# Routing into expert slots: gathering by the one-hot matrix itself, the norm's factor applied by slot, and the first expert slabs taken by halves

## The chip, the cores and the metric

The kernel runs on one core of one Trainium2 chip. The metric is device time in microseconds of one execution; "before" was run three times, and the median is used. Engines are called TensorE (PE; PEld is its weight load), VectorE (DVE), ScalarE (ACT), GpSimd (POOL) and SyncE (SP), which issues the DMAs.

## The reference, cut to what matters

One encoder layer over 256 tokens of width 1024, all in float32: a first RMSNorm and one wide projection, two attention branches, gates and an output projection, a residual sum. Then the part that this change is about:

```python
h2 = rmsnorm(x, norm_ffn_g)                 # x * rsqrt(mean(x*x) + eps) * gain
group_logits = h2 @ w_router_group + b      # 8 groups
g_sel = argmax(group_logits); w_grp = softmax(group_logits)[g_sel]
exp_logits = (h2 @ w_router_expert + b).reshape(t, 8, 4)
top_vals, top_idx = top_k(exp_logits[g_sel], 2)
combine = one_hot(4 * g_sel + top_idx) * softmax(top_vals) * w_grp
for e in range(32):
    out += (silu(h2 @ w_gate[e]) * (h2 @ w_up[e])) @ w_down[e] * combine[:, e]
x = x + out                                 # and a final RMSNorm
```

The weights of the 32 experts are 96 MB of the 134 MB that the kernel reads.

## The kernel before, in words

The 256 tokens are two tiles of 128 (`t` = 0, 1). The attention half projects with weights split into a high and a low part (three products each, L301 to L303), and ends with `out_product`, whose sums plus the input give `x2` (L809). Weights come in slabs of up to 128 x 2048 float32 (1 MB). Each expert has two slabs for gate and up (the first and the second 512 of the 1024 inputs, `c` = 0, 1), and each group of four experts has four slabs for down, so a group is 12 slabs and all groups are 96. The slabs land in 24 places of SBUF, in order. `take()` (L232) hands out the next slab and issues, on SyncE, the loads whose place has been used up: slab 24 goes where slab 0 was and waits for the last product that reads slab 0.

Routing runs between the attention half and the experts. For each token tile the transposed `x2` is made on TensorE (`turned`, L819) and copied out (L827, L829); eight products per tile give the 40 logits in one PSUM bank per tile (`logits`, L836, banks `lgp[0]` and `lgp[1]`). `inv_root` makes the norm's factor `r2` on VectorE from a square root on ScalarE. `chosen(t)` is a chain of nine small VectorE operations (L850 to L868), each waiting for the one before; its first reads the logits and `r2`, its last gives `sel`, the two chosen experts of each token. Products with a triangle matrix (`cums`, L974, L975, L982) count the tokens ahead of each token at its expert; `place_of` (L879) makes the slot number from it, and `slots` (L884) the one-hot matrix `P_` (tokens by 4 experts x 32 slots) of one group. A second operation (L887) multiplies it by `r2` to `Pr`; it runs on VectorE for group 0, and on GpSimd for the others. `gather` (L902) multiplies `x2` by `Pr`, so a group's tokens come transposed, four of the eight 128-row blocks in each of two banks `gx`; `kept_tokens` (L907) copies them out with the gain.

Then, for each expert, two `gate_up` (L1054: 8 matmuls, shown as 16 instructions) fill one bank, `kept` copies it out (L1060), `hidden` folds it (L1070) and applies Silu (L1075, L1076). After four experts the next group is gathered, `places` (L1019 to L1038) prepares the way back, and four `down` (L1095) and `combine` (L297, L1109) add the group's result to the banks `OA`, which `residual` (L917) has started with `x2`. `heat` (L310) is a product whose result nobody reads; it writes columns 256 to 511 of a bank.

The order on TensorE is the written one from the last output products on (`manual_schedule`, L928). On ScalarE and VectorE it is written by hand in two stretches, L945 to L991 and L1179 on; `in_turn` takes one operation of each of its chains in turn. `weigh` (the combine weights: exponentials on ScalarE, sums on VectorE) is written in the loop, at expert 0. The order of the other engines is made by a planner.

Of the kernel before, what the change touches and what calls it, by code (L numbers as in the profile page):

```python
# [26 lines left out]
CAP = 32  # L27
# [51 lines left out]
def block_kernel(ctx: ExitStack, tc: tile.TileContext, a, out, cap=CAP):  # L79
# [795 lines left out]
    Pr = wk.tile([128, 2, GRP], F32, tag="P0", name="Pr", bufs=1)  # L875
# [5 lines left out]
    def slots(grp, t, eng):  # L881
# [6 lines left out]
        yield  # L888

    def placed(t, cum):  # L890
        place_of(t, cum)
        yield
        yield from slots(0, t, nc.vector)
# [4 lines left out]
    def gather(c, t, p):  # L898

        for k in range(4 * c, 4 * c + 4):  # L900
            kk = k - 4 * c
            nc.tensor.matmul(p[:, kk * GRP:(kk + 1) * GRP], x2[:, t, k * 128:(k + 1) * 128], Pr[:, t],  # L902
                             start=(t == 0 and kk == 0), stop=(t == 1 and kk == 3))

    def kept_tokens(c, p):

        nc.vector.tensor_mul(tokens[c], p.rearrange("p (k s) -> p k s", k=4), bc(g_ffn[:, 4 * c:4 * c + 4], GRP, axis=2))  # L907
# [3 lines left out]
    def residual(i):  # L911

        t, h, c = i // 4, i // 2 % 2, i % 2
        if c == 0:
            OA[t][h] = pa("OA")
        c0 = 256 * c
        nc.tensor.matmul(OA[t][h][:, c0:c0 + 256], ident, x2[:, t, h * 512 + c0:h * 512 + c0 + 256], start=c == 0,  # L917
                         stop=False)

# [25 lines left out]
    urgent.enter_context(tc.manual_schedule(engines={mybir.EngineType.Activation, mybir.EngineType.DVE}))  # L945
# [48 lines left out]
    wts, wg = sm([128, 2, NE], "wts"), sm([128, 2], "wg")  # L994

    def weigh():
        neg = sm([128, 2, 2], "neg")
        nc.vector.tensor_scalar(neg[:, 0], gm, -1.0, None, op0=ALU.mult)
        nc.vector.tensor_scalar(neg[:, 1], m8[:, :, 0], -1.0, None, op0=ALU.mult)
        ge, se = sm([128, 2, NG], "ge"), sm([128, 2], "se")  # L1000
        for t in range(2):
            nc.scalar.activation(ge[:, t], gl[:, t], AF.Exp, bias=neg[:, 0, t:t + 1], accum_out=wg[:, t:t + 1])
            nc.scalar.activation(wts[:, t], el[:, t], AF.Exp, bias=neg[:, 1, t:t + 1])
        for t in range(2):
            nc.vector.scalar_tensor_tensor(wts[:, t], wts[:, t], 1.0, sel[:, t], op0=ALU.mult, op1=ALU.mult,
                                           accum_out=se[:, t:t + 1])
        nc.vector.tensor_mul(se, se, wg)
        nc.vector.reciprocal(se, se)
        for t in range(2):
            nc.vector.tensor_scalar(wts[:, t], wts[:, t], se[:, t:t + 1], None, op0=ALU.mult)  # L1010
# [31 lines left out]
    quarters = [slice(32 * j, 32 * j + 32) for j in range(4)]  # L1042

    def gate_up(n, c, w):
# [134 lines left out]
    with in_order, tc.manual_schedule(engines={mybir.EngineType.Activation, mybir.EngineType.DVE}):  # L1179
        for grp in range(NG):  # L1180
            if grp + 1 < NG:
                for t in range(2):
                    for _ in slots(grp + 1, t, nc.gpsimd):
                        pass
            for e in range(EPG):
# [13 lines left out]
                if n == 0:  # L1199
                    weigh()  # L1200
# [3 lines left out]
                if n == 1:  # L1204
                    for i in range(4, 8):
                        residual(i)
            if grp + 1 < NG:
                for c in range(2):
                    p = pss("gx")
                    for t in range(2):  # L1210
                        gather(c, t, p)
                    kept_tokens(c, p)
            hidden(EPG * grp + EPG - 1)()
            places(grp)()
# [123 lines left out]
```

## Time and profile before

| | us |
|---|---|
| median of three runs | 420.94 (420.42 to 422.38) |
| the profiled execution | 420.53 |
| its span (first to last instruction) | 418.7 |
| TensorE busy | 390.6, 93% of the span |
| VectorE, ScalarE busy | 208.2, 184.4 |
| data read from HBM | 133.4 MB, 321 GB/s over the span |

The table is to be read with the slices over time, since the shares are means over stages of different kinds: a busy TensorE in the attention half and a busy TensorE among the experts need not bound the kernel both. A line of the timeline gives start, duration, engine, line, operation, what it writes and reads, its shape, how many instructions are merged in it, and in brackets how long the engine sat idle before it and what released it. In a merged line the duration runs from the first start to the last end.

### The profile page before, as it was taken

The numbers are of one execution on the slowest core, as the hardware profiler recorded it, in microseconds if no ns is written. First come the engines' busy times: TensorE is split into PE (matmuls) and PEld (weight loads), VectorE is DVE, ScalarE is ACT, GpSimd is POOL, SyncE is SP. The second block draws the span as 40 slices with busy tenths as digits, with TensorE's granted clock in tenths as the row PEclk, the third lists the DMA queues.
The fourth block names the chain that finished last, engine by engine and source line by source line (L and its number), as shares of the span: only waits on it lengthen the run. The fifth ranks groups of instructions, "written<-read, shape, count | busy, mean of one in ns | idle before, by whom it ended". The sixth has DMA issues, their size and how long they took to land.

```text
span 418.7 us, 8153 instructions
## 1 busy us (share of the span) xinstructions
PE 390.6 (93%) x3280; PEld 286.7 (68%) x3280; DVE 208.2 (50%) x554; ACT 184.4 (44%) x403; POOL 27.0 (6%) x30
## 2 busy tenths in 40 slices
PE   7999999999999999999999999999999797797780
PEld 4888887888877878888885757576766373363440
DVE  2989689989869855765571212130303021020023
ACT  4876687668857846565432212212112111111143
POOL 0890000000000000000000010101001001000000
PEclk9999999999999999999999999999999999799996
DMA  7985683649543859589857999999999999999962
GB/s 266 396 359 196 250 310 110 257 160 372 208 160 145 312 206 386 198 312 360 308 229 316 423 419 420 420 422 417 420 420 419 421 420 419 421 420 420 418 259 106
DMA packets 20639, 135.00 MB, mean 322 GB/s; under 512 B 2418, under 2 KB 2930, under 8 KB 5620
## 3 DMA queue, kind: packets, MB, share of 16 engines
q1 hardware_dynamic: 20596, 134.42, 80.9%
q8 instruction: 28, 0.46, 0.5%
q14 instruction: 15, 0.12, 0.1%
HBM read 133.36 MB, written 1.05 MB: 321 GB/s over the span
## 4 chain that ended last, share of the span: by engine, by line
PE 75%; DMA 20%; DVE 2%; ACT 1%; issue 0%; SPq 0%; DVEq 0%; ACTq 0%
DMA w<-in_w_moe 19%; PE a L301 13%; PE a L302 13%; PE a L303 13%; PE G L1054 9%; PE gx L902 5%; PE Y L1095 5%; PE OA L1109 3%; PE G L1070 3%; PE s L318 2%; DMA w<-in_w_att 1%; PE t L543 1%; PE t L455 1%; PE o L603 1%; PE o L659 1%; PE t L647 1%
## 5 line engine op out<-in xcount | busy, mean ns | idle before, releaser
L302 PE MATMUL a<-r 128*128 128x512 f32 (+1 forms) x244 | 93.9, 387 | 0.0
L303 PE MATMUL a<-r 128*128 128x512 f32 (+1 forms) x244 | 92.4, 384 | 0.0
L301 PE MATMUL a<-r 128*128 128x512 f32 (+1 forms) x244 | 83.3, 387 | 1.5 <-ACT r L297 1.5
L1054 PE MATMUL G<-w,tok 128*32 128x256 f32 x1024 | 69.6, 399 | 14.0 <-DMA w<-in_w_moe 14.0
L297 DVE SCALAR_TENSOR_TENSOR r<-w,ident,r 128x512 fp32r<-128x512 f32 (+2 forms) x79 | 62.8, 807 | 15.6 <-ACT r L297 15.3
L297 ACT ACTIVATE r<-w,ident 128x512 fp32r<-128x512 f32 (+2 forms) x79 | 56.9, 750 | 27.1 <-PE a L303 24.8
L1054 PEld LDWEIGHTS G<-w,tok 128*32 128x32 f32 x1024 | 29.7, 112 | 40.3 <-issue 14.6
L301 PEld LDWEIGHTS a<-r 128*128 128x128 f32 x244 | 45.0, 188 | 10.7 <-ACT r L297 2.0
L302 PEld LDWEIGHTS a<-r 128*128 128x128 f32 x244 | 45.9, 188 | 8.6 <-DVE r L297 0.5
L303 PEld LDWEIGHTS a<-r 128*128 128x128 f32 x244 | 45.8, 188 | 8.3 <-issue 0.2
L1076 DVE TENSOR_TENSOR P<-G,P 128x64 f32<-128x64 f32 x32 | 7.2, 225 | 84.3 <-ACT P L1075 84.3
L1075 ACT ACTIVATE P<-G 128x64 f32<-128x64 f32 x32 | 7.2, 224 | 74.5 <-PE G L1070 74.4
L1060 ACT COPY Gs<-G 128x256 f32<-128x256 f32 x32 | 11.9, 372 | 48.4 <-PE G L1054 48.4
L1095 PE MATMUL Y<-w,P 128*32 128x256 f32 x512 | 30.9, 382 | 1.1 <-DMA w<-in_w_moe 1.1
L902 PEld LDWEIGHTS gx<-Pr,x 128*128 128x128 f32 x256 | 29.2, 192 | 3.5 <-issue 3.1
L902 PE MATMUL gx<-Pr,x 128*128 128x128 f32 x256 | 30.7, 278 | 0.2 <-DVE Pr L887 0.2
L297 DVE SCALAR_TENSOR_TENSOR ysb<-Y,ws,ysb 128x512 fp32r<-128x512 f32 (+1 forms) x18 | 12.5, 692 | 36.2 <-ACT ysb L297 19.6
L887 POOL TENSOR_SCALAR Pr<-P,r 128x128 f32<-128x128 f32 x14 | 8.3, 603 | 313.2 <-PE gx L902 188.7
L283 DVE TENSOR_TENSOR r<-w,r 128x512 fp32r<-128x512 f32 x32 | 21.9, 690 | 13.2 <-ACT r L282 10.2
L282 ACT CAST r<-w 128x512 fp32r<-128x512 f32 x32 | 19.8, 620 | 13.7 <-DVE r L283 8.2
L907 DVE TENSOR_TENSOR tok<-gx,ident 128x512 f32<-128x512 f32 x16 | 11.1, 692 | 26.5 <-PE gx L902 26.3
L1070 PEld LDWEIGHTS G<-cst,Gs 128*128 128x128 f32 x128 | 17.5, 199 | 9.8 <-issue 5.3
(222 smaller groups left out, 454.4 us busy)
## 6 DMA issues: line engine op xcount, KB each, us to landing
w<-in_w_moe SPq DMA_DIRECT2D x93, 1024.0 KB, 19.8
w<-in_w_att SPq DMA_DIRECT2D x24, 1024.0 KB, 4.8
w<-in_w_moe SPq DMA_DIRECT2D x6, 512.0 KB, 15.0
w<-in_w_att SPq DMA_DIRECT2D x3, 744.0 KB, 8.7
w<-in_w_att SPq DMA_DIRECT2D x2, 512.0 KB, 5.0
out<-r SPq DMA_DIRECT2D x2, 512.0 KB, 3.3
w<-in_w_att SPq DMA_DIRECT2D x1, 768.0 KB, 6.0
w<-in_w_att SPq DMA_DIRECT2D x2, 372.0 KB, 5.9
```

Source lines behind the costliest of these rows:

```text
L282: nc.scalar.copy(hi, src)
L283: nc.vector.tensor_sub(lo, src, hi.bitcast(F32))
L297: return nc.scalar.mul(hi, ps, g), nc.vector.scalar_tensor_tensor(lo, ps, g, hi.bitcast(F32), op0=ALU.mult, op1=ALU.subtract)
L301: i = nc.tensor.matmul(out_, lh, rh, start=start, stop=False)
L302: nc.tensor.matmul(out_, lh, rl, start=False, stop=False)
L303: nc.tensor.matmul(out_, ll, rh, start=False, stop=stop)
L902: nc.tensor.matmul(p[:, kk * GRP:(kk + 1) * GRP], x2[:, t, k * 128:(k + 1) * 128], Pr[:, t], start=(t == 0 and kk == 0), stop=(t == 1 and ...
L1054: nc.tensor.matmul(G[quarters[2 * z + o], :256], tokens[c][:, kk + o, CAP * e:CAP * e + CAP], w[:, (kk + o) * 512 + z * 256:(kk + o) * 512 ...
L1060: nc.scalar.copy(Gs, G[:, :256])
L1070: nc.tensor.matmul(HT[:, f * 64:(f + 1) * 64], Gs[:, f * 128:(f + 1) * 128], fold, start=True, stop=True)
L1095: nc.tensor.matmul(Y[quarters[e]], hT_[:, e, f], wv[:, f, e], start=f == 0, stop=f == 1)
L1109: nc.tensor.matmul(OA[t][h][:, c0:c0 + w], pl[:, t * 128:(t + 1) * 128], v, start=False, stop=grp == NG - 1 and q0 > 0 and v is lo, skip_g ...
```

## The change

Seven edits, all between the last output product and the second group of experts, but for one that touches every group.

The one-hot matrix is no longer multiplied by `r2`. `gather` uses `P_`; the factor is brought to the slots instead (`factors`: two products `P_` by `r2`, then `spread`: four products that lay it out for the four quarters of a bank), and `kept` of `gate_up` multiplies by it where it copied.

```diff
-        eng.tensor_scalar(Pr[:, t], P_[:, grp % 2, t], r2[:, t:t + 1], None, op0=ALU.mult)
+    rep = cp.tile([128, CAP], F32, name="rep")
+    nc.gpsimd.tensor_add(rep, fold[:, :CAP], fold[:, CAP:])
+    def factors(grp):
+        p = pss("rq")
+        for t in range(2):
+            nc.tensor.matmul(p[:, :1], P_[:, grp % 2, t], r2[:, t:t + 1], start=(t == 0), stop=(t == 1))
+        rd = wk.tile([128, EPG], F32, tag="rd", name="rd")
+        nc.vector.tensor_scalar(rd, own, p[:, :1], None, op0=ALU.mult)
+        def spread():
+            for q in quarters:
+                nc.tensor.matmul(p[q, 4:4 + EPG], rep, rd, start=True, stop=True)
+            rqs[grp] = wk.tile([128, EPG], F32, tag="rq", name="rq")
+            nc.vector.tensor_copy(rqs[grp], p[:, 4:4 + EPG])
+        return spread
-            nc.scalar.copy(Gs, G[:, :256])
+            nc.scalar.mul(Gs, G[:, :256], rqs[n // EPG][:, e:e + 1])
```

`gather` and `kept_tokens` can do a part: some of the blocks, and the slots of some of the experts. The routing's order is rewritten; `weigh` is split into `weigh` (the exponentials) and `weighed` (the sums), and two one-element activations, Exp and Silu, are put ahead of their first use.

```diff
+    root = inv_root(ss2[:, 1, 1:2], D, "n21", early[1], r2[:, 1:2], True)
+    logits(4, 4, 0)
     kept = turned(4, 4, 1, 4)
-    logits(4, 4, 0)
+    residual(0)
+    heat(lgp[0], 1)
     kept()
+    nc.scalar.activation(warm, ones[:, :1], AF.Exp)
     cums = [pt("cum") for _ in range(2)]
-    in_turn(inv_root(ss2[:, 1, 1:2], D, "n21", early[1], r2[:, 1:2], True), chosen(0))
+    chain = chosen(0)
+    next(chain)
+    in_turn(chain, root)
     logits(4, 4, 1)
-    residual(0)
-    residual(1)
-    heat(lgp[0], 6)
+    heat(lgp[0], 4)
...
-    residual(2)
-    residual(3)
-    heat(lgp[0], 5)
-    in_turn(chosen(1))
-    in_turn(placed(0, cums[0][:, :NE]))
+    residual(1)
+    chain = chosen(1)
+    for _ in range(3):
+        next(chain)
+    in_turn(chain, placed(0, cums[0][:, :NE]))
     gx = [pss("gx") for _ in range(2)]
+    gather(0, 0, 0, gx[0])
     nc.tensor.matmul(cums[1][:, :NE], tri, sel[:, 1], start=False, stop=True)
-    heat(lgp[0], 3)
-    gather(0, 0, gx[0])
-    gather(1, 0, gx[1])
+    gather(0, 1, 0, gx[1], 0, 2)
+    heat(cums[0], 2)
     in_turn(placed(1, cums[1][:, :NE]))
-    gather(0, 1, gx[0])
-    gather(1, 1, gx[1])
-    for c in range(2):
-        kept_tokens(c, gx[c])
+    gather(0, 0, 1, gx[0])
+    gather(0, 1, 0, gx[1], 2, 4)
+    weigh()
+    nc.scalar.activation(warm, ones[:, :1], AF.Silu)
+    for i in range(2):
+        kept_tokens(0, gx[0], 2 * i, 2)
```

The first two experts are taken by halves: both first slabs, then both second ones, and the two slabs change places in memory. The rest of the gather, the factors and the other residuals stand between.

```diff
-        off = i * 128 * 2048
+        off = {1: 2, 2: 1}.get(i, i) * 128 * 2048
+            if grp == 0:
+                gate_up(0, 0, take()[1])
+                gather(0, 1, 1, gx[1])
+                for i in range(2):
+                    kept_tokens(1, gx[1], 2 * i, 2)
+                spread = factors(0)
+                gate_up(1, 0, take()[1])
+                spread()
+                kept = gate_up(0, 1, take()[1])
+                for i in range(2, 4):
+                    residual(i)
+                kept()
+                weighed()
+                kept = gate_up(1, 1, take()[1])
+                hidden(0)()
+                kept()
...
-            for e in range(EPG):
+            for e in range(0 if grp else 2, EPG):
```

In the later groups `factors(grp + 1)` stands behind the gather and `spread()` between `hidden` and `places`, and in the loop's first group the slots of group 1 and the residuals 4 to 7 follow the part shown; `slots` of the next group runs on VectorE alone. The order of ScalarE and VectorE is now one stretch from L945 to the end of the loop.

## Rows read from the trace of the kernel before

**Rows 1.** The slices over time of the page: what the DMA engines moved in each of 40 equal parts of the span (10.5 us each).

```profile
GB/s 266 396 359 196 250 310 110 257 160 372 208 160 145 312 206 386 198 312 360 308 229 316 423 419 420 420 422 417 420 420 419 421 420 419 421 420 420 418 259 106
```

**Rows 2.** The chain of waits from its end: start, duration, what the end of the kernel waited for; the first and the last of the four pieces of DMA at its end.

```profile
320.54 19.87 DMA w<-in_w_moe
...
380.22 18.68 DMA w<-in_w_moe
```

**Rows 3.** Half-microsecond windows around the stop of the DMA: length, then the busy time of PE, PEld, DVE, ACT and POOL with the count of instructions in brackets, then the granted TensorE clock, the DMA engines' share and GB/s. The rows from 221.5 and from 229.5 are the first and the last of the 17 windows from 221.5 to 230.

```profile
214.50:215.00 0.50, 0.50 (x6) 0.36 (x4) 0.43 (x5) 0.00 (x0) 0.00 (x0) 1.00 0.93 360
...
216.50:217.00 0.50, 0.50 (x7) 0.50 (x7) 0.39 (x4) 0.33 (x3) 0.00 (x0) 1.00 0.00 0
...
221.50:222.00 0.50, 0.50 (x16) 0.33 (x12) 0.00 (x0) 0.25 (x1) 0.00 (x0) 1.00 0.88 147
...
223.00:223.50 0.50, 0.50 (x10) 0.29 (x12) 0.00 (x0) 0.28 (x1) 0.00 (x0) 1.00 0.99 410
...
229.50:230.00 0.50, 0.50 (x7) 0.46 (x4) 0.00 (x0) 0.00 (x0) 0.00 (x0) 1.00 1.17 492
```

**Rows 4.** The timeline from the gather to the first `down`.

```profile
215.98 3.84 PE L902 MATMUL gx<-Pr,x 128*128 128x128 f32 x32 [0.15 <-DVE Pr L887]
...
218.97 0.69 DVE L907 TENSOR_TENSOR tok<-gx,ident 128x512 f32<-128x512 f32 x1
...
219.75 2.80 PE L1054 MATMUL G<-w,tok 128*32 128x256 f32 x48
...
220.88 20.16 SPq L215 DMA_DIRECT2D w<-in_w_moe  x13
...
223.07 1.07 PE L1054 MATMUL G<-w,tok 128*32 128x256 f32 x16
...
223.22 1.28 ACT L1075 ACT_TABLE_LOAD   x1 [1.09 <-PE G L1070]
...
236.15 3.62 PE L1095 MATMUL Y<-w,P 128*32 128x256 f32 x61
```

**Rows 5.** The chain of waits through the routing.

```profile
208.68 0.82 PE s L836 x8
...
209.50 0.46 PE t L819 x4
...
209.96 0.83 PE s L836 x8
...
224.14 1.06 PE OA L917 x4
```

**Rows 6.** The timeline of the routing.

```profile
205.02 0.42 DVE L829 COPY x2T<-t 128x256 f32<-128x256 f32 x1 [1.36 <-ACT x2T L827]
...
208.71 0.59 ACT L827 COPY x2T<-t 128x512 f32<-128x512 f32 x1 [0.30 <-PE t L819]
...
210.82 0.26 DVE L850 SCALAR_TENSOR_TENSOR lg<-s,r,b_r 128x40 f32<-128x40 f32 x1 [0.47 <-PE s L836]
...
212.80 0.18 DVE L868 TENSOR_SCALAR sel<-el 128x32 f32<-128x32 f32 x1
...
212.89 0.25 DVE L850 SCALAR_TENSOR_TENSOR lg<-s,r,b_r 128x40 f32<-128x40 f32 x1
...
213.15 0.31 PE L974 MATMUL cum<-sel,cst 128*128 128x32 f32 x2
...
214.86 0.18 DVE L868 TENSOR_SCALAR sel<-el 128x32 f32<-128x32 f32 x1
...
215.09 0.41 PE L982 MATMUL cum<-sel,cst 128*128 128x32 f32 x2
```

**Rows 7.** The timeline of `places` of group 0.

```profile
236.12 0.19 PE L1026 MATMUL pl<-sel,cst 128*1 128x32 f32 x1
...
236.35 0.37 ACT L1030 CAST pl<-pl 128x256 fp32r<-128x256 f32 x1 [0.83 <-PE pl L1026]
...
236.76 0.16 DVE L1033 SCALAR_TENSOR_TENSOR wsx<-pl,cst 128x4 f32<-128x4 f32 x1 [0.97 <-ACT pl L1030]
```

**Rows 8.** Single lines of the kernel: duration of one in ns (least, median, most), first and last start, shape.

```profile
L310 PE MATMUL s<-ident_r x14: 272/273/273, 212.5 to 215.6; 128*128 128x256 bf16 x14
...
L884 DVE TENSOR_TENSOR P<-cst,place x16: 281/285/292, 215.2 to 350.6; 128x128 f32<-128x128 f32 x16
...
L1060 ACT COPY Gs<-G x32: 368/372/373, 221.8 to 396.4; 128x256 f32<-128x256 f32 x32
...
L297 ACT ACTIVATE ysb<-Y,ws x18: 473/687/688, 238.1 to 407.8; 128x512 fp32r<-128x512 f32 x14, 128x256 fp32r<-128x256 f32 x4
```

**Rows 9.** The chain of waits at the `down` of group 1.

```profile
256.41 3.59 PE Y L1095 x64
```

**Rows 10.** One-microsecond windows in the last third, with the columns of rows 3.

```profile
332.00:333.00 1.00, 0.00 (x0) 0.00 (x0) 0.00 (x0) 0.04 (x1) 0.00 (x0) 1.00 1.00 418
...
333.00:334.00 1.00, 0.90 (x12) 0.60 (x16) 0.00 (x0) 0.00 (x0) 0.00 (x0) 0.58 1.02 426
...
347.00:348.00 1.00, 0.09 (x4) 0.10 (x8) 0.00 (x0) 0.32 (x1) 0.00 (x0) 1.00 1.00 418
...
348.00:349.00 1.00, 1.00 (x17) 0.42 (x17) 0.00 (x0) 0.00 (x0) 0.00 (x0) 1.00 1.02 426
```

**Rows 11.** The timeline of TensorE at 333.

```profile
333.10 1.94 PE L1054 MATMUL G<-w,tok 128*32 128x256 f32 x16 [1.51 <-DMA w<-in_w_moe]
```

More of the change, by code (lines that the diff above doesn't have):

```diff
@@ L874, in block_kernel, with slots @@
     hT_ = shaped(P_and_hT[:, 4 * GRP:], [128, EPG, 2, CAP])
-    Pr = wk.tile([128, 2, GRP], F32, tag="P0", name="Pr", bufs=1)
+    rep = cp.tile([128, CAP], F32, name="rep")
+    nc.gpsimd.tensor_add(rep, fold[:, :CAP], fold[:, CAP:])
+    rqs = {}
+    quarters = [slice(32 * j, 32 * j + 32) for j in range(4)]
+    def factors(grp):
[10 more added lines that the diff above has]
+        return spread
     def place_of(t, cum):
         nc.vector.scalar_tensor_tensor(place[:, t], cum, 1.0, sel[:, t], op0=ALU.add, op1=ALU.mult)
-    def slots(grp, t, eng):
+    def slots(grp, t):
         dst = P_[:, grp % 2, t].rearrange("p (e s) -> p e s", e=EPG)
@@ L892, in placed, with gather, kept_tokens @@
         yield
-        yield from slots(0, t, nc.vector)
+        yield from slots(0, t)
     tokens = [wk.tile([128, 4, GRP], F32, tag=f"gt{z}", name="tok", bufs=1) for z in range(2)]
-    def gather(c, t, p):
-        for k in range(4 * c, 4 * c + 4):
+    def gather(grp, c, t, p, k0=0, k1=4):
+        for k in range(4 * c + k0, 4 * c + k1):
             kk = k - 4 * c
-            nc.tensor.matmul(p[:, kk * GRP:(kk + 1) * GRP], x2[:, t, k * 128:(k + 1) * 128], Pr[:, t],
+            nc.tensor.matmul(p[:, kk * GRP:(kk + 1) * GRP], x2[:, t, k * 128:(k + 1) * 128], P_[:, grp % 2, t],
                              start=(t == 0 and kk == 0), stop=(t == 1 and kk == 3))
-    def kept_tokens(c, p):
-        nc.vector.tensor_mul(tokens[c], p.rearrange("p (k s) -> p k s", k=4), bc(g_ffn[:, 4 * c:4 * c + 4], GRP, axis=2))
+    def kept_tokens(c, p, e0=0, n=EPG):
+        es = slice(CAP * e0, CAP * (e0 + n))
+        nc.vector.tensor_mul(tokens[c][:, :, es], p.rearrange("p (k s) -> p k s", k=4)[:, :, es],
+                             bc(g_ffn[:, 4 * c:4 * c + 4], CAP * n, axis=2))
     OA = [[None, None], [None, None]]
@@ L944, in block_kernel @@
     urgent.enter_context(tc.high_priority(300))
-    urgent.enter_context(tc.manual_schedule(engines={mybir.EngineType.Activation, mybir.EngineType.DVE}))
+    by_trace = ctx.enter_context(ExitStack())
+    by_trace.enter_context(tc.manual_schedule(engines={mybir.EngineType.Activation, mybir.EngineType.DVE}))
     added(512, 512, 0, acc[1])
@@ L1041, in block_kernel @@
     pls, Gss = {}, {}
-    quarters = [slice(32 * j, 32 * j + 32) for j in range(4)]
     def gate_up(n, c, w):
@@ L1177, in final_part @@
         nc.vector.tensor_mul(ob[:, t, c0:c0 + n], OA[t][h][:, cs], g_fin[0][:, c0:c0 + n])
-    with in_order, tc.manual_schedule(engines={mybir.EngineType.Activation, mybir.EngineType.DVE}):
+    with in_order, by_trace:
         for grp in range(NG):
-            if grp + 1 < NG:
+            if 0 < grp < NG - 1:
                 for t in range(2):
-                    for _ in slots(grp + 1, t, nc.gpsimd):
+                    for _ in slots(grp + 1, t):
                         pass
-            for e in range(EPG):
+            if grp == 0:
[14 more added lines that the diff above has]
+                kept()
+                for t in range(2):
+                    for _ in slots(1, t):
+                        pass
+                for i in range(4, 8):
+                    residual(i)
+            for e in range(0 if grp else 2, EPG):
                 n = EPG * grp + e
@@ L1203, in block_kernel @@
                     todo.pop(0)()
-                if n == 1:
-                    for i in range(4, 8):
-                        residual(i)
             if grp + 1 < NG:
@@ L1210, in block_kernel @@
                     for t in range(2):
-                        gather(c, t, p)
+                        gather(grp + 1, c, t, p)
                     kept_tokens(c, p)
+                spread = factors(grp + 1)
             hidden(EPG * grp + EPG - 1)()
+            if grp + 1 < NG:
+                spread()
             places(grp)()
```

36 lines of the change are left out of this document (17 added, 19 removed).

## The prediction

> **What bounds the kernel now.** I read the 40 slices first. From the 23rd slice on the DMA engines move 417 to 424 GB/s until the last two slices, while they were uneven before that [rows 1]. The chain of waits says the same from its end: from 320.54 to 398.90 it is nothing but waits for expert weights, the first of 19.87 us and the last of 18.68, and only then the last products run [rows 2]. So the second half of the kernel is one saturated stream. It has a start that can be seen. All 24 places of the ring are filled when routing begins to end: the half-microsecond windows show 360 GB/s until 215.0, nothing from 216.5 on, 147 again from 221.5, and full rate from 223.0 [rows 3]. The timeline gives the event that ends the gap: the first `gate_up` runs from 219.75, and SyncE's next expert load is issued at 220.88, behind the last product that read slab 0 [rows 4]. Summing the 17 windows from 221.5 to 230 gives 3.20 MB, which is 7.61 us at 420 GB/s; so the stream counts as full from 222.39, 1.56 us after the release (220.83, just ahead of the issue). Behind it come 72 slabs of 1.049 MB and the final gain of 0.52 MB: 76.0 MB, 181.0 us, and 222.4 + 181.0 = 403.4, where the tail begins. The end therefore moves one for one with the release of slab 0, less whatever the stream starves later. Work of the engines inside the stream is free as long as places come free faster than one per 1.049/0.42 = 2.50 us.
>
> All sums are against the profiled execution, 420.53 us (span 418.7 and 1.83 around it); the median of the runs shown is 420.94, 0.41 above, and the forecast is given on the median.
>
> **The chain to the release, step by step.**
>
> 1. *Logits before transposes.* Before, TensorE went from 209.50 through four transposes (0.46) to `logits(4, 4, 0)`, ending 210.79 [rows 5], and the first op of `chosen(0)` (L850) started at 210.82 [rows 6]. After, the logits go first; their copy (ScalarE, 208.71 + 0.59 = 209.30) [rows 6] is ready, so they end at 209.50 + 0.83 = 210.33. By this alone L850 gains 0.46.
>
> 2. *But an idle product is put between.* `heat(lgp[0], 1)` now stands ahead of `chosen(0)` and writes columns 256 and up of the same PSUM bank that L850 reads in columns 0 to 39. Does L850 wait for it? The trace has the like case: in `places`, ScalarE's copy L1030 reads columns 0 to 255, done by L1019, yet starts at 236.35, just as the products L1026 into columns 272 and up end (236.31); and VectorE's L1033, which reads columns 256 to 259 of that bank, starts at 236.76, released by the end of the ScalarE copy [rows 7]. So this program orders its engines by bank and not by column. The bounds are no wait at all (210.36) and the whole wait; I take the whole wait, since all the rows of this kind show it. TensorE then passes the transposes (0.46), `residual(0)` (two of the four instructions that took 1.06 [rows 5], 0.53) and one idle product (0.27 [rows 8]) before L850: 210.33 + 1.26 + 0.03 = 211.62, which is 0.80 later than before. This is the largest single number of my sum, and it goes against the change.
>
> [...]
>
> 3. *`chosen(0)` and `chosen(1)`.* L850 to the end of L868 takes 2.16 (210.82 to 212.98), with three ops of the second root between already [rows 6]; so the first choice is ready at 213.78, and the second L850 starts 0.09 behind the start of L868, at 213.69. Its own logits don't hold it: the copy behind the transposes ends near 211.4, and eight instructions more take until 212.4.
>
> 4. *First slots early.* Before, VectorE did all nine ops of `chosen(1)` and then the slots, ending with a product by the norm's factor; gather began at 215.98 [rows 4]. After, `cums[0]` is there 0.48 after the choice (212.98 to 213.46), at 214.26; `place_of` slips in behind L857 at 214.5, the slots start 0.22 to 0.3 later at 214.8 and take 0.28 [rows 8]. Gather starts at 215.15, 0.83 earlier. Price: the slots occupy VectorE in front of L862, which could cost nothing or their whole 0.28; I take 0.1, so the second choice is ready at 213.69 + 2.15 + 0.1 = 215.93, 0.89 later than before (215.04).
>
> 5. *Second half.* TensorE does a quarter of the gather (3.84/4 = 0.96) to 216.11, then `cums[1]` (0.41 [rows 6]) to 216.52. VectorE's place and slots take 0.04 + 0.22 + 0.28: 217.1. The quarter that completes `gx[0]` runs to 218.1. Before, both banks had to pass in the order (0,0), (1,0), (0,1), so it ended at 218.86.
>
> 6. *Tokens by halves of the slots.* Before, 0.11 of waiting, one product of 0.69 and 0.09 to TensorE. After, the first half of 256 columns costs about 0.42 (the same size copied from PSUM by VectorE took 0.42 [rows 6]; the ends are half of 0.69 and the whole). 218.1 + 0.11 + 0.42 + 0.09 = 218.7, against 219.75. **The release moves by -1.0 us.** If the first `gate_up` waited for both halves, one more half of at least 0.35 would come on top: -0.65.
>
> **What stands against it later: the first places come free more slowly.** Slab 1 is now the next expert's half, but between the first two `gate_up` stand the last quarter of the gather (0.96) and `factors` (four short products with 128 rows and columns of weights; like the gather's, 0.12 each, 0.48). Release to release is 0.96 + 0.48 + 0.93 (a third of the 2.80 for 48 products) = 2.37, just under the 2.50 that a slab lasts. Up to the first `down` the new work on TensorE is that 1.44, two `spread` of eight instructions (like those of `down`, 61 in 3.62, so 0.47 each), two residuals moved in (0.53 each) and `factors(1)` (0.48): 3.9 in all. Before, this stretch took from 220.83 to 237.05 (16 of the 61 products behind 236.15), 16.2 [rows 4]; after 20.1, and the stream needs the ninth place after 8 x 2.50 = 20.0. So it misses by 0.1, which I take; the lower bound is 0, the upper 0.7 if the instructions in front of VectorE's answers also wait.
>
> **Costed at nothing.** Groups 1 to 7 gain `factors` and `spread`, 0.95 each, 6.7 in all; hidden, since TensorE goes from one group's `down` to the next in 20.3 us (236.15 to 256.41) while 12 slabs take 30 [rows 4, 9]; bounds 0 and 6.7. The 14 GpSimd products vanish; nobody on the chain waited for them. The gate and up copy with a factor may cost 0.47 in place of 0.37 (copies of 128x256 with and without one [rows 8]), on a ScalarE whose results TensorE does not lack: what it waits for there are weights [rows 2]. The table loads, 1.28 each, are off the chain: Silu's at 223.22 delayed ScalarE alone, while TensorE went on with products [rows 4]. The new places have cover too (Exp from 211.4, wanted at 217; Silu from 218.4, wanted at 222); without it each is worth up to 1.28. The weights' sums move past the tokens of group 0, and are needed 15 us later. The swap of two slabs in memory changes the order in which equal transfers come.
>
> **Sum:** -1.0 + 0.1 = -0.9 on 420.53, 419.6; on the median **420.0 us**. About 0.5% (2.1 us) is what a measurement here tells from no change.
>
> **Rivals.**
> - *A: L850 does not wait for the idle product.* Then steps 3 to 6 start 1.25 earlier (210.36), and the release moves by -2.25; with 0.1 of starving, 418.8. For it: the columns are apart, and no row shows this very pair in this order. Against: both waits of [rows 7]. Chance 0.20.
> - *B: the clock falls, slower than before.* Seven idle products and two residuals fewer stand in the routing, and TensorE now waits from 212.9 to 213.9 for the first choice, with a shorter gap at 215. [...] If it fell near 215, the two gather quarters, `cums[1]` and the first `gate_up` (0.96 + 0.96 + 0.41 + 1.0 = 3.3) would take twice that, since 16 instructions of `gate_up` took 1.94 at 333.10 [rows 11] against 1.07 at 223.07 [rows 4]: 420.0 + 3.3 = 423.3. It decides from the point where the clock falls before the release. Against it: one gap of a microsecond, with dense work on both sides. Chance 0.07.
> - *C: the stream starves at the ninth place*, by 1.1, because `spread`, `factors` and the tokens interleave worse than their instructions add up. The gain is eaten: 420.94 - 1.0 + 1.1 = 421.0. For it: the sum leaves 0.1. Chance 0.13.
>
> [...]
>
> **How the numbers follow.** The forecast has 0.60; its own range is 419.4 to 420.7 (the wait of step 2 whole, starving 0 to 0.7, the half token and the slots either way). A and C are taken into the range, B is left out: 418.5 to 421.4. Faster by over 0.5% means under 418.84: half of A and a little of the forecast, 0.14. Slower by over 0.5% means over 423.04: most of B, 0.06. Within: 0.80.
>
> **What would show it.** In the profile after: L850's first start near 211.6 behind an idle product, not 210.4 (step 2 against A); gather from 215.1 in three parts; the first `gate_up` at 218.7; the DMA gap about 1 us shorter; full rate at the ninth place near 239 (against C); granted clock 1.00 from 210 to 225 (against B). I am wrong if the release moves by more than 1.6 or less than 0.4, or if the stream is no longer saturated behind it.

## The result, and the profile after

The changed kernel takes 423.54 us (median of 7 runs, 421.86 to 424.27); the kernel before took 420.51 beside it (420.30 to 422.38). The ratio is 1.0061, 95% interval 1.0043 to 1.0079: slower by 1.8 to 3.3 us; the medians lie 3.0 apart. Forecast were 420.0 and a range of 418.5 to 421.4, with a chance of 0.06 for slower. The profiled execution took 424.17 us, its span 421.9 (2.27 around it); before it was 420.53, 418.7 and 1.83.

The slices of the changed kernel's page, beside [rows 1]: the stream dips in the 24th slice (393, 419 before), and then is steady near 418 in place of 420. The 22nd slice reads 387 where it read 316, but mostly because a slice of the longer span lies 1.7 us later there: in this execution the first load behind the stop is issued at 220.74 us, only 0.14 ahead of the kernel before (220.88).

```profile
GB/s 271 383 372 209 228 298 141 259 169 330 200 200 124 339 212 324 208 361 345 332 149 387 416 393 420 416 419 419 418 419 418 414 419 419 418 419 419 413 192 105
```

Its chain of waits from the end, beside [rows 2]: the same wait for weights, ending 2.75 us later (401.78 against 399.03 in the kernel before, whose line stands second). So 2.75 of the 3.2 us by which this span is longer lie in the stream, or ahead of it, and 0.5 in the tail.

```profile
362.99 19.89 DMA w<-in_w_moe
382.94 18.71 DMA w<-in_w_moe
401.78 0.64 PE Y L1125 x8
```

```profile
399.03 0.64 PE Y L1095 x8
```

The timeline of the routing, beside [rows 4, 6]. This execution runs 0.33 us ahead of that of the kernel before when routing begins (the first transposes behind attention start at 207.74 and 208.07). L851 (L850 before) is released by the idle product L311, as step 2 said. But the first quarter of the gather, 8 instructions, takes 2.05 us, twice the 0.96 that a quarter took before, and the first `gate_up` comes at 219.61 and not at 218.7.

```profile
210.84 0.27 PE L311 MATMUL s<-ident_r 128*128 128x256 bf16 x1
211.15 0.26 DVE L851 SCALAR_TENSOR_TENSOR lg<-s,r,b_r 128x40 f32<-128x40 f32 x1 [1.34 <-PE s L311]
...
213.41 0.38 PE L1021 MATMUL cum<-sel,cst 128*128 128x32 f32 x2 [0.65 <-PE s L311]
...
214.84 2.05 PE L920 MATMUL gx<-P,x 128*128 128x128 f32 x8 [0.16 <-DVE m8s L863]
...
219.61 1.07 PE L1084 MATMUL G<-w,tok 128*32 128x256 f32 x16
```

One-microsecond windows of that stretch (columns as in [rows 3]) say why: the granted clock falls to 0.50. In the four microseconds from 211 to 215, in the last of which it falls, TensorE was busy for 0.87, 0.76, 0.59 and 0.84.

```profile
211.00:212.00 1.00, 0.87 (x8) 0.76 (x7) 0.82 (x7) 0.98 (x2) 0.00 (x0) 1.00 1.00 410
212.00:213.00 1.00, 0.76 (x7) 0.46 (x6) 0.93 (x8) 0.69 (x2) 0.00 (x0) 1.00 1.06 442
213.00:214.00 1.00, 0.59 (x5) 0.62 (x6) 0.86 (x7) 0.00 (x0) 0.00 (x0) 1.00 1.01 426
214.00:215.00 1.00, 0.84 (x4) 0.31 (x4) 0.96 (x6) 0.00 (x0) 0.00 (x0) 0.62 0.64 254
215.00:216.00 1.00, 1.00 (x5) 1.00 (x6) 0.44 (x4) 0.00 (x0) 0.00 (x0) 0.50 0.06 25
...
217.00:218.00 1.00, 1.00 (x7) 0.98 (x8) 0.64 (x4) 0.17 (x1) 0.00 (x0) 0.68 0.00 0
218.00:219.00 1.00, 1.00 (x11) 1.00 (x10) 0.00 (x0) 0.98 (x7) 0.00 (x0) 1.00 0.00 0
```

That is rival B's place, but it turned out not to be the main loss. To compare executions, times below are counted from the first transpose behind attention (208.07 before). "Release" is the first of SyncE's expert loads behind it, "ninth" the ninth, "GB/s" the DMA rate from 255 to 395 us, "end" the end of the span, "around" what the profiled execution took beside its span; the ratio is to the kernel before on the same chip. All columns but the last two come from one profiled execution of each kernel.

| kernel | first gate_up | release | ninth | GB/s | end | around | median us | ratio (95%) |
|---|---|---|---|---|---|---|---|---|
| before | 11.68 | 12.81 | 29.19 | 420 | 210.6 | 1.83 | 420.5 | |
| after | 11.86 | 13.00 | 32.84 | 418 | 214.2 | 2.27 | 423.54 | 1.0061 (1.0043 to 1.0079) |
| e13_again | 10.64 | 11.78 | 31.62 | 418 | 213.0 | 2.23 | 423.93 (one) | |
| e14_again | 10.64 | 11.77 | 31.62 | 418 | 213.3 | 2.29 | 424.19 (one) | |
| e1_heat | 10.59 | 11.72 | 31.56 | 418 | 212.7 | 2.20 | 421.92 | 1.0041 (1.0020 to 1.0063) |
| e2_late | 10.64 | 11.77 | 29.35 | 418 | 211.4 | 2.24 | 422.13 | 1.0049 (1.0031 to 1.0066) |
| e3_both | 10.59 | 11.72 | 29.29 | 418 | 210.6 | 2.14 | 421.30 | 1.0020 (1.0006 to 1.0035) |
| e4_load | 11.67 | 12.81 | 32.68 | 420 | 213.0 | 1.79 | 422.79 | 1.0049 (1.0032 to 1.0066) |
| e5_pad | 11.67 | 12.80 | 29.18 | 418 | 211.6 | 1.84 | 421.68 | 1.0016 (1.0000 to 1.0031) |
| e6_align | 11.67 | 12.80 | 29.18 | 425 | 208.4 | 1.82 | 418.51 | 0.9933 (0.9910 to 0.9955) |
| e7_rep | 10.59 | 11.72 | 29.29 | 420 | 209.8 | 2.22 | 420.38 | 0.9991 (0.9977 to 1.0004) |
| e8_bank | 10.42 | 11.56 | 29.13 | 420 | 209.5 | 2.16 | 420.13 | 0.9982 (0.9965 to 1.0000) |
| e9_afterrep | 10.66 | 11.79 | 31.64 | 420 | 212.6 | 2.12 | 422.37 | 1.0036 (1.0023 to 1.0049) |
| e10_order | 9.75 | 10.88 | 28.45 | 420 | 209.5 | 2.29 | 420.56 | 0.9991 (0.9979 to 1.0003) |
| e11_best | 9.74 | 10.87 | 28.44 | 425 | 206.7 | 1.76 | 418.03 | 0.9933 (0.9919 to 0.9946) |
| e12_pad32 | 11.67 | 12.81 | 29.19 | 420 | 210.7 | 1.81 | 420.84 | 1.0000 (0.9991 to 1.0009) |
| e15_pad160 | 10.64 | 11.77 | 31.62 | 425 | 209.7 | 2.12 | 420.44 | 0.9979 (0.9969 to 0.9989) |
| e16_pad416 | 11.67 | 12.80 | 29.18 | 425 | 208.6 | 1.85 | 418.65 (one) | |
| e17_pad224 | 11.67 | 12.80 | 29.19 | 419 | 210.9 | 1.80 | 420.70 (one) | |

### The profile page after: what moved, and what is told of

Same layout as the page of the kernel before. It is cut to its first block, busy times and chain, and to the rows that moved or that the text cites. A ratio compares the mean times of both kernels' runs of the same rounds, so it can differ in the third digit from the quotient of the medians.

```text
span 421.9 us, 8323 instructions
## 1 busy us (share of the span) xinstructions
PE 395.4 (94%) x3369; PEld 291.5 (69%) x3369; DVE 210.2 (50%) x570; ACT 188.6 (45%) x405; POOL 18.9 (4%) x17
## 4 chain that ended last, share of the span: by engine, by line
PE 59%; DMA 34%; DVE 4%; ACT 1%; issue 1%; SPq 0%; DVEq 0%; ACTq 0%
DMA w<-in_w_moe 32%; PE a L302 12%; PE a L303 12%; PE a L304 12%; PE G L1084 4%; PE gx L920 3%; PE Y L1125 2%; PE s L319 2%; PE OA L1139 1%; DMA w<-in_w_att 1%; PE G L1100 1%; PE t L544 1%; PE OA L937 1%; PE t L456 1%; PE o L604 1%; PE o L660 1%
## 5 line engine op out<-in xcount | busy, mean ns | idle before, releaser
L1084 PE MATMUL G<-w,tok 128*32 128x256 f32 x1024 | 67.1, 388 | 11.2 <-DMA w<-in_w_moe 11.1
L1090 ACT ACTIVATE Gs<-G,rq 128x256 f32<-128x256 f32 x32 | 15.2, 474 | 46.2 <-PE G L1084 46.2
L920 PEld LDWEIGHTS gx<-P,x 128*128 128x128 f32 x256 | 30.6, 198 | 4.0 <-issue 4.0
L920 PE MATMUL gx<-P,x 128*128 128x128 f32 x256 | 32.6, 285 | 0.2 <-DVE m8s L863 0.2
L298 DVE SCALAR_TENSOR_TENSOR ysb<-Y,ws,ysb 128x512 fp32r<-128x512 f32 (+1 forms) x18 | 12.4, 691 | 36.3 <-ACT ysb L298 19.5
L283 ACT CAST r<-w 128x512 fp32r<-128x512 f32 x32 | 19.8, 622 | 13.7 <-PE a L304 7.8
L926 DVE TENSOR_TENSOR tok<-gx,ident 128x512 f32<-128x512 f32 (+1 forms) x18 | 11.2, 632 | 29.2 <-PE gx L920 29.2
L1125 PEld LDWEIGHTS Y<-w,P 128*32 128x32 f32 x512 | 15.1, 109 | 11.5 <-DMA w<-in_w_moe 1.4
```

The lines of the kernel that those rows point to most:

```text
L283: nc.scalar.copy(hi, src)
L298: return nc.scalar.mul(hi, ps, g), nc.vector.scalar_tensor_tensor(lo, ps, g, hi.bitcast(F32), op0=ALU.mult, op1=ALU.subtract)
L926: nc.vector.tensor_mul(tokens[c][:, :, es], p.rearrange("p (k s) -> p k s", k=4)[:, :, es], bc(g_ffn[:, 4 * c:4 * c + 4], CAP * n, axis=2))
L1084: nc.tensor.matmul(G[quarters[2 * z + o], :256], tokens[c][:, kk + o, CAP * e:CAP * e + CAP], w[:, (kk + o) * 512 + z * 256:(kk + o) * 512 ...
L1090: nc.scalar.mul(Gs, G[:, :256], rqs[n // EPG][:, e:e + 1])
L1125: nc.tensor.matmul(Y[quarters[e]], hT_[:, e, f], wv[:, f, e], start=f == 0, stop=f == 1)
```

## Experiments: the clock and the ninth place

Theory 1 was the clock's fall; theory 2 that the stream starves because its ninth place opens late.

**e1_heat** puts idle products where TensorE had thinned out.

```diff
-    heat(lgp[0], 4)
+    heat(lgp[0], 11)
...
     residual(1)
+    heat(lgp[0], 4)
```

> The changed kernel with 11 idle products (not 4) ahead of the first count and 4 more behind residual 1, so that TensorE is not idle while VectorE makes the two choices. Theory 1 (half clock from 214.4 to 217.7 held the gather up): granted clock 1.00 throughout the routing, the first quarter of the gather takes 1.0 in place of 2.05, the first gate_up starts 1.2 us earlier (about 218.4), and the time falls by about 1.2 us against the changed kernel, to about 422.3. Theory 2 (the stream starves at the ninth place, whatever the release) alone: the release moves, the ninth place with it, and the stream still loses 2 us there. Rival: the clock falls all the same, and nothing moves.

421.92 us, 1.6 under the changed kernel's median and near the 422.3 of theory 1 (by the two ratios the gain is 0.8 us, and their intervals overlap). In the profile the clock stayed at 1.00, and the release came 1.09 earlier than in the kernel before: step 6's -1.0. The kernel stayed 1.3 us slower than before, so the clock was not the whole loss.

**e2_late** moves six residuals out of the way of the ninth place; **e3_both** has both edits.

```diff
-                for i in range(2, 4):
-                    residual(i)
...
-                for i in range(4, 8):
-                    residual(i)
...
+            if grp == 0:                  # behind the first `down`
+                for i in range(2, 8):
+                    residual(i)
```

> The changed kernel with the residual products 2 to 7 (six, about 3 us of TensorE) behind the first group's down in place of between the first releases. Theory 2: the ninth place comes free about 3 us earlier, the DMA engines stay at 420 GB/s between 240 and 250, and the time falls by about 2 us against the changed kernel, to about 421.5. Rival (the loss is all in the release and the clock): no difference, 423.5.

> Both edits: more idle products in the routing and the residual products 2 to 7 behind the first down. If theories 1 and 2 together are the whole loss, about 1.2 + 2 = 3.2 us less than the changed kernel, 420.3, at or just under the kernel before; and since the release is then 1.0 earlier than before, as the forecast had it, 419.6 if nothing else is lost. Rival (a third loss in the long stream): 421 or more.

e3_both took 421.30 us, 1 us over its expectation. Its profiled span ends 2.1 earlier than that of e1_heat, whose release is the same; its median is only 0.6 lower. What differs is the ninth place: 29.29 against 31.56. e2_late took 422.13, 1.4 under the changed kernel's median but 0.6 over its expectation, although its ninth place is as early (29.35) and its clock stayed at 1.00. Its profiled span ends 0.8 later than that of e3_both; a reading of the landings below says where.

**e4_load** is to make the ninth place late in the kernel before, with nothing else of the change.

```diff
+                    heat(pss("idle"), 32)   # behind residuals 4 to 7 of group 0
```

> The kernel before with 32 idle products (about 3.5 us of TensorE, what the change puts there) behind residual 4 to 7 of the first group. Theory 2: the ninth place comes free about 20 us behind the first in place of 16.4, the DMA rate falls below 400 GB/s for some microseconds near 241, and the kernel is 1 to 2 us slower than before (421.5 to 422.5). Rival (supply of places has room there): no difference, 420.5.

422.79 us, 2.2 above its kernel before, and the profiled span ends 2.4 later. But it hit another place than it was meant to. The idle products stand ahead of the fifth release, too: the fifth load behind the stop is issued at 230.56, 9.73 behind the first (6.24 in the kernel before, 8.79 in e14_again), and the stream starves soon after, not near 241. When the ninth load is issued, at 240.70, the rate is full. The first four loads, the fifth, and three windows:

```profile
220.83 3.64 SPq L215 DMA_DIRECT2D w<-in_w_moe  x4
...
230.56 0.33 SPq L215 DMA_DIRECT2D w<-in_w_moe  x1
```

```profile
230.00:235.00 5.00, 5.00 (x72) 2.94 (x64) 0.45 (x2) 1.16 (x4) 0.00 (x0) 1.00 0.96 339
235.00:240.00 5.00, 5.00 (x55) 4.83 (x57) 1.57 (x3) 0.47 (x3) 0.00 (x0) 1.00 0.97 370
240.00:242.00 2.00, 2.00 (x44) 1.32 (x40) 0.40 (x4) 0.59 (x2) 0.00 (x0) 1.00 1.04 438
```

So e4_load shows that one late place behind the stop costs the kernel some 2 us, at a fifth place that by 4 x 2.50 = 10.0 was just in time. It does not test the ninth, which comes at 19.87 in a stream that is already late.

**e13_again and e14_again** are the changed kernel once more.

> The changed kernel as it is, for another look. In its first profile the clock was granted at 0.50 to 0.68 from 214 to 218 us and the first gate and up product came 11.70 us behind the last attention product; in e2_late and e9_afterrep, with the same routing, the clock stayed at 1.00 and it came at 10.48 and 10.50. If the fall belongs to the change's order of work: 0.50 again and 11.7. If it is a matter of the single execution: 1.00 in some looks, and 10.5.

> As e13_again, a third look at the changed kernel. Where the clock holds, the time should be about 1 us under that of a look in which it falls: 422.5 to 423 us beside 424.

In both the clock stayed at 1.00, with the same thin stretch (two windows of e14_again below), and the first `gate_up` came at 10.64. So the fall is a matter of the single execution: it cost the first profile 1.2 us at the release and about 1 us in the span, counted from the first transpose. The times, 423.93 and 424.19, were not lower, because the routing began 0.9 and 0.8 us later in these two executions (208.67 and 208.57 against 207.74). They show that the change costs some 3 us without a fall of the clock. How many of the seven runs behind the median had one is not known, since one of them was profiled.

```profile
214.00:215.00 1.00, 0.77 (x6) 0.74 (x6) 0.89 (x7) 0.00 (x0) 0.00 (x0) 1.00 1.01 410
215.00:216.00 1.00, 0.69 (x5) 0.37 (x4) 0.93 (x8) 0.00 (x0) 0.00 (x0) 1.00 0.65 270
```

The timeline of e14_again is therefore the one to hold against the forecast:

```profile
211.98 0.26 DVE L851 SCALAR_TENSOR_TENSOR lg<-s,r,b_r 128x40 f32<-128x40 f32 x1 [1.34 <-PE s L311]
...
215.66 1.13 PE L920 MATMUL gx<-P,x 128*128 128x128 f32 x8 [0.31 <-DVE m8s L863]
...
218.74 0.75 DVE L926 TENSOR_TENSOR tok<-gx,ident 128x256 f32<-128x256 f32 x2 [1.10 <-PE gx L920]
219.22 1.07 PE L1084 MATMUL G<-w,tok 128*32 128x256 f32 x16
```

Its SyncE queue has the first eight loads behind the stop in one stretch and the next four in another:

```profile
220.35 13.16 SPq L216 DMA_DIRECT2D w<-in_w_moe  x8
...
240.20 3.61 SPq L216 DMA_DIRECT2D w<-in_w_moe  x4
```

And its windows show the restart behind the release and the dip at the ninth place:

```profile
221.00:222.00 1.00, 1.00 (x16) 0.90 (x18) 0.59 (x2) 0.00 (x0) 0.00 (x0) 1.00 0.48 82
222.00:223.00 1.00, 1.00 (x32) 0.60 (x27) 0.43 (x4) 0.00 (x0) 0.00 (x0) 1.00 0.83 344
223.00:224.00 1.00, 1.00 (x14) 0.53 (x7) 0.90 (x9) 0.29 (x1) 0.00 (x0) 1.00 1.06 451
...
241.00:242.00 1.00, 1.00 (x24) 0.69 (x20) 0.21 (x1) 0.69 (x1) 0.00 (x0) 1.00 0.89 352
242.00:243.00 1.00, 1.00 (x28) 0.62 (x21) 0.54 (x1) 0.15 (x1) 0.00 (x0) 1.00 0.82 295
243.00:244.00 1.00, 1.00 (x14) 0.55 (x7) 0.00 (x0) 0.54 (x1) 0.00 (x0) 1.00 1.06 328
244.00:246.00 2.00, 2.00 (x21) 0.97 (x21) 1.15 (x3) 0.24 (x1) 0.00 (x0) 1.00 0.94 299
```

The kernel before moved 422 GB/s from 244 to 246:

```profile
244.00:246.00 2.00, 2.00 (x32) 1.19 (x28) 0.21 (x1) 0.22 (x1) 0.00 (x0) 1.00 1.03 422
```

Against 420, the five microseconds of e14_again from 241 lack 68 + 125 + 92 + 2 x 121 = 527 GB/s times us, 1.25 us of stream. In e3_both the same stretch of the stream is nearly whole:

```profile
242.00:244.00 2.00, 2.00 (x22) 1.09 (x20) 0.00 (x0) 0.00 (x0) 0.00 (x0) 1.00 0.99 397
244.00:246.00 2.00, 2.00 (x24) 1.09 (x20) 1.07 (x3) 0.00 (x0) 0.00 (x0) 1.00 1.05 434
```

The windows give a mean over the 16 DMA engines. The traces also hold sixteen landing times for each load, one for each part of it. In two pairs of executions the release and the rate are the same and the ninth place is not: e3_both and e1_heat, and e7_rep and e9_afterrep (described below), at 17.57 and 19.85 behind the release. From the eighth to the thirteenth load behind the stop, the mean of the sixteen moves on by 12.6 us in e3_both and 13.2 in e1_heat, by 12.5 in e7_rep and 13.7 in e9_afterrep; the last of the sixteen by 12.5 and 14.8, and by 12.4 and 15.1. In e14_again it is 13.8 in the mean, which is the 1.25 above, and 14.8 in the last part. So with the late ninth place the stream loses 0.6 to 1.3 us here in the mean, and 2.3 to 2.7 in the last part (in the first profile of the changed kernel 0.8 and 2.2, in e13_again 0.3 and 1.2).

The end goes by the last part. At the last load of expert weights it is 1.9 us later behind the release in e1_heat than in e3_both, the mean only 0.5; the span ends 2.1 later. In e2_late the mean there is 0.1 later than in e3_both, the last part 1.0: that is its 0.8. Why one part falls behind the others is open.

## Experiments: the place of the ring

e3_both left a loss: its release lay 1.09 ahead of the kernel before, yet its span ended level. Every run with the change moved 418 GB/s in the steady part, the kernel before and e4_load 420. The change's only tile ahead of the ring of weights is `rep`, 128 bytes a partition. In the compiled programs the ring's places, 8,192 bytes each, begin 352 bytes past a multiple of 512 before the change and 480 behind it.

**e5_pad, e6_align, e12_pad32, e16_pad416, e17_pad224** are the kernel before with an unused tile of 128, 160, 32, 416 and 224 bytes there.

```diff
+    pad = cp.tile([128, 32], F32, name="pad")    # 40, 8, 104, 56 in the others
+    nc.gpsimd.memset(pad, 0.0)
```

> The kernel before with one unused tile of 128 bytes a partition ahead of the ring of slabs, as the change has one (rep): every slab lands 128 bytes higher, and nothing else is changed. Between 255 and 395 us the kernel before moves 420 GB/s and every run that holds the change 418. Theory A (the place of the ring in the partitions sets how long a packet takes): 418 GB/s here too, eight slabs in 19.88 to 19.94 us in place of 19.80 to 19.87, the stream's end 0.7 us later, 421.2 to 421.4 us beside 420.6. Rival B (the changed work of the groups, the choice's slots on VectorE or the factors, slows the stream): 420 GB/s, 420.6 us.

> The kernel before with an unused tile of 160 bytes there, which sets the ring on a multiple of 512 bytes. Theory A says only that the place matters, not which is good: anything from 418 GB/s (421.3 us) to the 0.309 us a packet that the trace shows early in the stream, which would be 427 GB/s and 3 us less, 417.6 us; my guess is 420 GB/s and 420.6 us within 0.4. Rival B: 420 GB/s, 420.6 us.

> The kernel before with 32 unused bytes ahead of the ring: the slabs begin on a multiple of 128 bytes, but not of 512 (384 past one). If a multiple of 64 or 128 is what the packets want: 425 GB/s and 418.5 us as in e6_align. If it must be 512: 418 to 420 GB/s and 420.6 to 421.5 us.

> The kernel before with 416 unused bytes ahead of the ring: the slabs begin 256 bytes past a multiple of 512. The places tried so far gave 420 GB/s between 255 and 395 us (352 and 384 past one), 418 (480) and 425 (0). If a multiple of 256 is enough: 425 GB/s, some 418.5 us. If only 512 will do: 418 to 421 GB/s.

> The kernel before with 224 unused bytes ahead of the ring: the slabs begin 64 bytes past a multiple of 512. If a packet costs more the nearer its start lies to the end of a piece of 512 bytes (0: 425, 352 and 384: 420, 480: 418 GB/s), 64 lies between 420 and 425 GB/s; if everything off the multiple costs about the same, 418 to 420.

The window from 255 to 395 us, first of the kernel before, then of the changed kernel, of e5_pad, of e6_align and of e16_pad416:

```profile
255.00:395.00 140.00, 125.78 (x1510) 79.74 (x1508) 24.57 (x68) 24.37 (x65) 5.91 (x10) 0.96 1.01 420
```

```profile
255.00:395.00 140.00, 128.88 (x1588) 84.81 (x1586) 26.77 (x81) 26.86 (x65) 0.00 (x0) 0.99 1.01 418
```

```profile
255.00:395.00 140.00, 125.09 (x1506) 80.12 (x1505) 24.42 (x68) 24.20 (x64) 5.92 (x10) 0.96 1.01 418
```

```profile
255.00:395.00 140.00, 128.62 (x1534) 82.68 (x1533) 24.80 (x69) 24.82 (x66) 5.91 (x10) 0.95 1.01 425
```

```profile
255.00:395.00 140.00, 126.11 (x1534) 80.28 (x1534) 24.80 (x69) 24.80 (x66) 5.94 (x10) 0.98 1.01 425
```

e12_pad32 took 420.84 us at 420 GB/s: a multiple of 128 is not enough. So the rate goes with the start: 425 GB/s at 0 and 256 bytes past a multiple of 512, 419 at 64, 420 at 352 and 384, 418 at 480. By ratio, e5_pad loses 0.16% and e6_align gains 0.67%. I had guessed no gain for e6_align: a miss that became the largest single gain of the study, one tile of padding in the kernel before. e16_pad416 took 418.65 us and e17_pad224 420.70, one run each beside 420.85.

Against 425 GB/s the start at 64 lost 1.4% and the start at 480 1.7%. Why a start off a multiple of 256 costs this, no run shows.

**e9_afterrep** gives the change its old ring, **e15_pad160** an aligned one.

```diff
-    rep = cp.tile([128, CAP], F32, name="rep")
+    rep = wk.tile([128, CAP], F32, tag="rep", name="rep", bufs=1)    # e9_afterrep
+    rep = cp.tile([128, CAP + 8], F32, name="rep")[:, :CAP]          # e15_pad160
```

> The changed kernel with its tile rep put behind the ring, so that the slabs land where the kernel before has them; all else of the change stays. If the three costs add up as I read them (a late ninth place, slower packets, some 0.4 us around the span), this takes the packets' part away alone: 420 GB/s between 255 and 395 us in place of 418, 0.7 us less than the changed kernel, 422.6 to 423.0 us. If the stream's rate costs nothing while slabs starve: 423.5 as the changed kernel.

> The changed kernel with 32 more bytes in rep's tile, which sets the ring on a multiple of 512 bytes, nothing else: 425 GB/s between 255 and 395 us in place of 418, which over the 156 us of the stream is 2.5 us less than the changed kernel (423.5): 420.6 to 421.2 us, level with the kernel before in spite of the late ninth place. If starving slabs eat the faster packets: 422 us or more, with the rate between 240 and 250 us under 390 GB/s.

422.37 and 420.44 us: as expected within 0.3. The dip at the ninth place stays in both.

## Experiments: towards a better version

**e7_rep** is e3_both with `rep` behind the ring; **e8_bank** also drops `heat(lgp[0], 1)`; **e10_order** has 4 idle products ahead of the first count in place of e8_bank's 11; **e11_best** is e10_order with the ring on a multiple of 512 and a small copy on GpSimd in each group.

```diff
-    heat(lgp[0], 1)                                  # e8_bank
...
-    heat(lgp[0], 11)                                 # e10_order
+    heat(lgp[0], 4)
...
+    rep = cp.tile([128, CAP + 8], F32, name="rep")[:, :CAP]     # e11_best
...
+            nc.gpsimd.tensor_copy(spare, rqs[grp])
```

> The run e3_both (idle products for the clock, the residuals late) with the tile rep put behind the ring, so that the ring is where the kernel before has it. Theory A: 420 GB/s, the stream's end 0.7 us earlier than in e3_both, 420.5 to 420.7 us beside its 421.3. Rival B: 418 GB/s and 421.3 us, as e3_both.

> e7_rep without the one idle product that writes the bank of the first logits. The choice's first operation, which waited for that product (0.65 us later behind the last attention product than in the kernel before), begins 0.8 to 0.9 us earlier, the first release 0.8 us earlier, and the stream with it: 0.8 us less than e7_rep, 419.8 us if theory A holds there, with the DMA rate between 240 and 250 us at 410 GB/s or more. Rival: the ninth place opens by TensorE's own work and the stream starves by what the release gained: as e7_rep. If TensorE's clock falls in the gap that the product filled, 1 to 1.5 us more than e7_rep.

> e8_bank with 4 idle products ahead of the first count in place of 11. In e8_bank the first choice was done at 213.15 us and its count waited for the 11 products until 214.21; with 4 it begins at 213.5. The second choice's chain on VectorE, done at 215.96, then sets the rest: its count at 215.97 in place of 216.43, so the first gate and up product and the first release 0.45 us earlier than in e8_bank, 419.7 us. If the clock falls with fewer idle products, 421 us or more; if the release gains and the ninth place does not follow, 420.1 us with a dip below 405 GB/s between 235 and 250 us.

> e10_order with the ring on a multiple of 512 bytes (rep and 32 bytes of padding ahead of it), and one copy of 8 columns by GpSimd in each group, which nothing waits for. The ring: 425 GB/s and 2.4 us less, as e6_align against the kernel before. The copies are for the 0.37 us that all kernels with the change have around the span (2.17 us beside 1.80): theory, GpSimd that has nothing to do after the first groups costs it at the end, so 1.80 here; rival, it has another cause, 2.17 here. In all 417.0 to 417.4 us, which would be under both kernels.

e7_rep took 420.38: the ring again. e8_bank took 420.13, not 419.8: L851 did begin when the logits ended, but the count behind the choice had to pass the 11 idle products that e1_heat had put there. Its timeline:

```profile
210.99 0.26 DVE L851 SCALAR_TENSOR_TENSOR lg<-s,r,b_r 128x40 f32<-128x40 f32 x1 [0.34 <-PE s L837]
...
212.97 0.18 DVE L869 TENSOR_SCALAR sel<-el 128x32 f32<-128x32 f32 x1
213.01 1.37 PE L311 MATMUL s<-ident_r 128*128 128x256 bf16 x11
...
214.21 0.31 PE L1020 MATMUL cum<-sel,cst 128*128 128x32 f32 x2
```

e10_order released 0.68 earlier still (more than the 0.45 expected), but its end and its time, 420.56, did not follow. In its profiled execution the mean landing of the last load did follow the release, 184.0 behind it against 184.1 in e8_bank, but the last of the sixteen parts came 1.0 later; for the median of its twelve runs the reason stays open. e11_best took 418.03, 0.6 over its expectation, under both kernels and level with e6_align (418.51). Its copies answered their question: 1.73 to 1.83 us around the span in its six runs, as in the kernel before, against 2.10 to 2.29 in all other kernels with the change. The ring is not what did it, since e15_pad160, aligned but without the copies, has 2.12 to 2.28. GpSimd left without work in the later groups costs 0.4 us outside the span; by what mechanism, no view shows.

## Why the prediction was wrong

**The failed step is the one on the ninth place: "the stream needs the ninth place after 8 x 2.50 = 20.0. So it misses by 0.1."** The term was sized at 0.1 (0 to 0.7). In the profiled executions it measured 2.1 and 2.8: with equal releases and equal rates the span ends 2.1 later in e1_heat than in e3_both, and 2.8 later in e9_afterrep than in e7_rep; in each pair the ninth load comes 19.85 against 17.57 behind the release (16.38 in the kernel before). The medians give 0.6 for the first pair and 2.1 for the second, each kernel taken against its own kernel before. So that it starves there is shown, and its size is 0.6 to 2.8.

The sum of instructions was good (20.1 forecast, 19.85 measured); what was wrong is the room. A room of 20.0 supposes that a load does its work as soon as it is issued and that all sixteen parts run out at once. In e14_again it takes from 220.35 to 223 until the rate is full, the sixteen parts of the eighth load land 2.1 us apart, and the dip begins in the window from 241, about one microsecond from the issue of the ninth load. The ninth place has its true limit between 17.57 and 19.85. The fifth, with a room of 10.0 by the same working, has it between 8.79 (e14_again, where the fifth load lands as in e3_both) and 9.73 (e4_load, where it starves). So rival C was the right mechanism, by the profiled spans at about twice its price, because I let a margin of 0.1 decide where the doubt about the room was of the order of a microsecond.

**Two terms were not in the sum.** The ring's shift by 128 bytes costs 0.7 us (e5_pad against the kernel before by ratio, with an interval that begins at no loss; e7_rep against e3_both 0.8 in the span, with the rate back at 420). No row shows an address, so I read `rep` only as a tile. "The 14 GpSimd products vanish; nobody on the chain waited for them" holds inside the span and misses the 0.4 us around it.

**What came true.** Step 2: L851 waits for the idle product, 3.41 behind the first transpose in e14_again and 3.41 in the changed kernel's first profile (3.55 forecast: 211.62 less 208.07); e8_bank, without the product, began 2.40 behind it. Steps 3 to 6: the release at -1.03 in e13_again and e14_again, -1.0 forecast. The factors and `spread` of the later groups stayed hidden: e9_afterrep, which has them all, moves 420 GB/s from 255 to 395. Two slips in the working changed nothing: the slices reach 423 and not 424, and the stretch taken as 16.2 is 16.38 between the issues.

**The sum again.** Against the kernel before, e9_afterrep ends its span 2.0 later (the early release in it), the ring adds 0.4 to 0.7 (e13_again, e14_again), GpSimd 0.4: 2.8 to 3.1, for a difference of medians of 3.0. These are single profiled executions. By medians e9_afterrep, GpSimd's part in it, is 1.55 above its kernel before, and the ring adds 0.7: 2.3 of the 3.0. The 0.7 left is within the intervals of the two ratios; whether the clock has a share in it is open.

**Rivals.** A did not happen. B's clock fell in one of three profiled executions and cost that one about 1 us; the two others lose the 3 us without it, and its share in the median is open (e1_heat's median is 1.6 lower). In [rows 10] the granted clock reads 0.58 behind a microsecond without a product, and 1.00 behind one with a busy share of 0.09; here it fell behind windows of 0.59 to 0.87, and in e14_again, with windows down to 0.59, it stayed at 1.00. No run shows what decides. B's price of 3.3 was too high, since the stretch at 0.50 to 0.68 ended by 218, before the first `gate_up` at 219.61. C decided most of it.

## What to carry to other kernels

A stream that stops and restarts needs its later places well before the earlier ones have run out (a room of 20.0 by bytes was enough here for a ninth place at 17.57, and not for one at 19.85): count the first places as less work than their bytes, and treat a margin under a microsecond as a loss until a run shows otherwise (0.15 and 0.27 lost here, 1.2 held). The end of such a stream goes by the slowest part of its loads, which the mean rate hides (in e1_heat the last load is 1.9 us later than in e3_both by its last part, 0.5 by its mean, and the span ends 2.1 later). When a change adds a tile, see where it pushes the tiles that DMA writes, and keep those on multiples of 256 bytes (425 GB/s here at 0 and 256 bytes past a multiple of 512, 418 to 420 at the four other starts). Before a single profile's clock is blamed, profile the same kernel again (here 0.50 in one of three executions, 1.00 in the two others).

## What was not expected of the hardware

The same program under the same routing kept the granted clock at 1.00 in the routing in two profiled executions (e13_again, e14_again), and it fell to 0.50 in a third, with no single idle gap on TensorE above 0.65 us (ahead of L1021). The start of an 8,192-byte place within 256 bytes changed the DMA rate by 1.2 to 1.7% (418 to 420 GB/s in place of 425). One small copy on GpSimd in each of the eight groups took 0.4 us off the time outside the span (1.73 to 1.83 us in e11_best, 2.10 to 2.29 in the other kernels with the change). And in one stream the last of a load's sixteen parts can lose 2.3 us where their mean loses 0.6 (e1_heat beside e3_both).
